# The next block's output product placed ahead of the last channel group of each feed-forward layer, with the sums kept in DRAM

## The chip, the core and the metric

The kernel runs on one core of a Trainium2 chip. A core has a matrix engine (PE, with weight loads listed as PEld), a vector engine (DVE), a scalar engine (ACT), a general engine (POOL), a queue engine that mostly issues DMAs (SP), and 16 DMA engines that all queues share. The engines run side by side, each in the order of its own instruction list, and wait for one another on semaphores. The metric is the device time of one execution in microseconds; lower is better.

## What is computed

One layer of a hybrid decoder trunk over 2048 tokens with 1024 features:

```python
h = rmsnorm(x, norm1_g) * (1 + sc1) + sh1
p = h @ w_in                                   # 3456 columns
y = concat([rglru(p), hgrn2(p), rwkv7(p)]) * mix_beta
x = x + g1 * (y @ w_out)                       # the output product
h = rmsnorm(x, norm2_g) * (1 + sc2) + sh2
x = x + g2 * ((silu(h @ w_gate) * (h @ w_up)) @ w_down)   # feed-forward, 2816 channels
return rmsnorm(x, final_g)
```

The three mixers (RG-LRU, HGRN2, RWKV-7) are recurrences along the tokens. They run in chunks, as many small operations on DVE and ACT with short matmuls between them.

## The kernel before, in words

Data lie feature-major: a tile has 128 features on the partitions and 512 tokens along the free side. The tokens are cut into four blocks (`NB`) of 512; the 1024 features are eight tiles (`KC`), the 2816 feed-forward channels 22 tiles (`NF`).

**Products.** Every f32 operand is split into a high part and a rest (`hh`/`hl` for activations, `wh`/`wl` for weights), and `project` (L261) makes three matmuls for each tile of the sum: high by high, high by rest, rest by high. An output product of one feature tile `d` is 8 x 3 = 24 matmuls, a down product over four channel tiles is 12, one over two channel tiles is 6. Weights come from DRAM by the SP queue into `wr` (3 buffers) and are split by ACT (`wh`) and DVE (`wl`, 4 buffers each). The products of `project` go to the PSUM banks `pd`, of which there are 3.

**Buffers that matter here.** `xs` is a tag with 12 buffers of one tile each (L135). From it come the loaded `x` tiles, the running sums `x1` of a block (eight tiles held from the output product to the final norm), squares and partial sums of squares, the scaled tiles in `make_h`, the gate results in `ffn_up`, and the loaded mixer outputs in `load_y`. `hh`/`hl` have 16 each.

**Order.** The program is written in Python and unrolled. A scheduler then orders each engine's instructions by a priority (levels `out`, `load`, `feed`, `mix`, `dense`, from first to last) as their inputs and buffers come free in its own model of the time. Tiles of one tag share its buffers; an instruction that first writes a tile needs a free buffer of the tag.

**Stages.** First the input projections and norms of all four blocks run, two blocks at a time (`w_in_products`), with the mixers of the first blocks interleaved. The last five projection columns (`IN_ORDER[-NT:]`) of blocks 2 and 3 end this stage. Then, for each block `b`:

- `w_out_products` (L1054): for each `d`, load the weight and the tile of `x`, make the product, add it to the tile with one DVE operation (`stt`), square it on ACT, and keep a sum of squares. At the end `rstd_of` (L354) turns the sum into the norm's factor: a split, matmuls with ones on PE, a logarithm and an exponential on ACT with a table load ahead of each.
- `ffn` (L1084): `make_h` (L388) scales and splits the eight tiles; then channel tiles are made by `ffn_up` (gate and up products) and consumed in groups of four, and a last group of two, by down products that add to `x1`. `load_y(b + 1)` (L1044) fetches the mixer outputs of the next block ahead of the last two groups; their split has the rest computed on POOL.
- `final_norm` of block `b` is deferred: it is called as `before()` inside the next block's `w_out_products`, behind the first product (L1063). It frees the eight `x1` tiles of block `b` as they are stored to `out`.

So in the order of PE the last down group of block `b` is followed by the output products of block `b + 1`, these by the norm's few matmuls, and these by the first up products of block `b + 1`, which need `make_h`.

Of the kernel before, what the change touches and what calls it, by code (L numbers as in the profile page):

```python
# [10 lines left out]
F = mybir.dt.float32  # L11
# [3 lines left out]
OP = mybir.AluOpType  # L15
PSUM = bass.MemoryType.PSUM

T = 2048
D = 1024
FF = 2816  # L20
TB = 512
KC = D // 128
NB = T // TB
NF = FF // 128
# [11 lines left out]
IN_ORDER = (25, 26, 19, 16, 20, 17, 22, 23, 7, 4, 10, 13, 0, 2, 21, 18, 24, 8, 5, 11, 14, 1, 3, 9, 6, 12, 15)  # L36
# [38 lines left out]
def hybrid_kernel(ctx, tc, x, par, ada_w, w_in, rgw, igw, w_up, a_up, g_up, w_out,  # L75
                  w_gate, w_upf, w_down, cst, msk, out):
    nc = tc.nc
    G, PE, SP = nc.gpsimd, nc.tensor, nc.sync
# [11 lines left out]
    @contextmanager  # L90
    def level(name):

        clock[levels[-1]] = tc.cur_priority
        levels.append(name)
        tc.cur_priority = clock[name]
        yield
        clock[name] = tc.cur_priority
        levels.pop()
        tc.cur_priority = clock[levels[-1]]
# [4 lines left out]
    def stt(o, a, s, b, op0, op1):  # L104
        return V.scalar_tensor_tensor(o, a, s, b, op0=op0, op1=op1)
# [19 lines left out]
    def bank(tag, bufs):  # L125
        return pp.tile([128, 512], F, name=tag, bufs=bufs)
# [17 lines left out]
    def pc(name, i=0):  # L144
        a, b = PCOLS[name]
        assert a + i < b
        return P[:, a + i:a + i + 1]
# [5 lines left out]
    def raw_w(src):  # L153
        w = dp.tile([128, TB], F, name="wr", bufs=3)
        i = SP.dma_start(w[:, :src.shape[1]], src)
        if w_after:
            order(i, w_after.pop())
        return w
# [30 lines left out]
    A2, B2, G1, G2 = Q2[:, 0:8], Q2[:, 8:16], Q2[:, 16:24], Q2[:, 24:32]  # L189
# [57 lines left out]
    def w_parts():  # L247
        return dp.tile([128, TB], R, name="wh", bufs=4), dp.tile([128, TB], R, name="wl", bufs=4)

    def load_w(src, fn):  # L250
        ws = []
        with level("load"):
            for c in range(0, src.shape[1], TB):
                n = min(TB, src.shape[1] - c)
                w = raw_w(src[:, c:c + n])
                hi, lo = w_parts()
                fn(w[:, :n], hi[:, :n], lo[:, :n])
                ws.append((hi, lo))
        return ws

    def project(h, *cols):  # L261

        ps = [bank("pd", 3) for ws in cols]
        tot = 3 * len(h)
        with level("dense"):
            for k, (hh, hl) in enumerate(h):
                c = slice((k % 4) * 128, (k % 4 + 1) * 128)
                for p, ws in zip(ps, cols):
                    wh, wl = ws[k // 4]
                    for n, (a, b) in enumerate(((wh, hh), (wh, hl), (wl, hh)), 3 * k):  # L270
                        PE.matmul(p, a[:, c], b, start=(n == 0), stop=(n == tot - 1))  # L271
                    now[0] += 0.68
                if k % (4 // len(ps)) == 4 // len(ps) - 1 or k == len(h) - 1:
                    tick()
        return ps
# [6 lines left out]
    def tick():  # L282
        for s in streams:
            while s["block"] < NB and now[0] >= s["at"]:
                step(s)
# [51 lines left out]
    def square_sum(s, t, k, tile=None, n=1):  # L337

        s, *last = s or (None,)
        if len(last) == n:  # L340
            if s is None:
                s = last.pop(0)
            else:
                (G if tile else V).tensor_add(s, s, last.pop(0))
        q = (tile or xs_)()
        if k == KC - 1:
            V.tensor_mul(q, t, t)
        else:
            squared[:] = [act(q, t, AF.Square)]
        return s, *last, q  # L350
# [18 lines left out]
    def load_x(src, b, k, tile=None):  # L369
        t = (tile or xs_)()  # L370
        load(t, src[k, :, b * TB:(b + 1) * TB])
        return t
# [39 lines left out]
    def drain(it):  # L412
        for _ in it:
            pass
# [3 lines left out]
    with level("feed"):  # L418
# [12 lines left out]
        rs = rstd_of(xsum)  # L431
# [20 lines left out]
    with level("mix"):  # L452
# [51 lines left out]
        for i in range(2):  # L504
            h, o = slice(64 * i, 64 * i + 64), slice(64 - 64 * i, 128 - 64 * i)
# [495 lines left out]
    def w_in_products(h, cols, side):  # L1001

        n = 0
        while n < len(cols):

            cs_ = cols[n:n + 2] if n == 0 and len(h) == 1 else cols[n:n + 1]
            ws = [W.pop(c) if c in W else load_w(w_in[c], split_v) for c in cs_]
            for i, b in enumerate(h):
                for j, (c, p) in enumerate(zip(cs_, project(h[b], *ws))):
                    with level("feed"):  # L1010
                        t = xs_()
                        if (n + i + j) % 2:
                            act(t, p)
                        else:
                            V.tensor_copy(t, p)
                        SP.dma_start(pd[c, :, b * TB:(b + 1) * TB], t)
                        stored.add((c, b))
                    next(side, None)
            n += len(cs_)
# [19 lines left out]
    for f in (mixers_a, mixers_b):  # L1039
        s = {"block": 0, "at": 0.0}  # L1040
# [3 lines left out]
    def load_y(b):  # L1044
        finish(b)
        ys = []
        for k in range(KC):
            t = load_x(yd, b, k)
            y = parts_()
            split(t, *y)  # L1050
            ys.append(y)
        return ys

    def w_out_products(b, ys, before):  # L1054
        x1, s = [], None
        for d in range(KC):
            ws = load_w(w_out[d], split_v)
            t = load_x(x, b, d)
            p, = project(ys, ws)
            with level("out"):  # L1060
                stt(t, p, G1[:, d:d + 1], t, OP.mult, OP.add)
            if d == 0:
                before()  # L1063
            s = square_sum(s, t, d)
            x1.append(t)
        return x1, rstd_of(s)

    def ffn_up(h, f):
        if f:
            p, = project(h, load_w(w_gate[f], split_v))  # L1070
        else:
            p, pu = project(h, load_w(w_gate[f], split_v), load_w(w_upf[f], split_v))
        t = xs_()
        with level("out"):
            act(t, p, AF.Silu)
        if f:
            pu, = project(h, load_w(w_upf[f], split_v))
        with level("out"):
            V.tensor_mul(t, pu, t)
        g = parts_()  # L1080
        split_v(t, *g)
        return g

    def ffn(b, x1, rs):  # L1084
        h = make_h(lambda k: x1[k], rs, A2, B2, "silu_and_others", over=False)
        gs, s, ys = [], None, None
        for f0 in range(0, NF, 4):
            n = min(4, NF - f0)
            while len(gs) < min(f0 + n + (2 if f0 + n + 2 >= NF else 1), NF):
                gs.append(ffn_up(h, len(gs)))  # L1090
            if len(gs) == NF and ys is None and b + 1 < NB:
                ys = load_y(b + 1)
            for d in range(KC):
                p, = project(gs[f0:f0 + n], load_w(w_down[d][:, f0 * 128:(f0 + n) * 128], split_v))
                with level("out"):
                    stt(x1[d], p, G2[:, d:d + 1], x1[d], OP.mult, OP.add)
                if f0 + n == NF:
                    s = square_sum(s, x1[d], d, n=1 if b + 1 < NB else 2)

        def final_norm():  # L1100
            rs = rstd_of(s)
            for d in range(KC):
                with level("dense"):
                    stt(x1[d], x1[d], pc("final_g", d), rs, OP.mult, OP.mult)
                    SP.dma_start(out[d, :, b * TB:(b + 1) * TB], x1[d])

        return ys, final_norm

    side = ada_rest()
    NH, NT = 4, 5  # L1110
    for b0 in range(0, NB, 2):
        h = {b0: h0}
        if b0 + 1 < NB:
            head, rest = IN_ORDER[:NH], IN_ORDER[NH:-NT]
            w_in_products(h, head, ahead)
            drain(ahead)
            h1 = {b0 + 1: norm1(b0 + 1)}
            w_in_products(h1, head, side)
            h.update(h1)
            ahead = x_stats(range(b0 + 2, min(b0 + 4, NB)), 1)  # L1120
            w_in_products(h, rest, chain(islice(side, 16), ahead, side))
            drain(ahead)
            w_in_products({b0: h[b0]}, IN_ORDER[-NT:], side)
            if b0 + 2 < NB:
                h0 = norm1(b0 + 2)
            w_in_products(h1, IN_ORDER[-NT:], side)
        else:
            w_in_products(h, IN_ORDER, side)
    drain(side)
    with level("feed"):  # L1130
        ys, before = load_y(0), lambda: None
    for b in range(NB):
        with level("feed"):
            ys, before = ffn(b, *w_out_products(b, ys, before))
    before()


# [54 lines left out]
```

## Time and profile before

| | us |
|---|---|
| median of 3 runs | 2858.53 |
| lowest, highest | 2855.87, 2863.30 |
| the profiled execution | 2862.48 |
| its span, first to last instruction | 2860.70 |

The profile is that of one execution, 3.95 us above the median of the runs; 1.8 us of it lie outside the span. Views of it group instructions by line and tile, list an engine's instructions in order of time, or give the busy time of each engine in a stretch. Nearly all instructions have line 69, a helper that counts them; they are told apart by their tiles. The DMA issues of the SP queue are listed with the time at which the queue issued them. The rows that matter stand in the prediction.

### The profile page before, as it was taken

How to read it: one execution, taken by the hardware profiler on the slowest of the kernel's cores; microseconds unless marked ns; L12 is line 12 of the kernel's file. 1: busy time of each engine (PE TensorE's matmuls, PEld its weight loads, DVE VectorE, ACT ScalarE, POOL GpSimd, SP SyncE). 2: the span in 40 equal slices, each digit the busy share in tenths (PEclk: the TensorE clock that was granted, in tenths of full speed). 3: DMA queues.
4: the chain of work that ended last, by engine and by line, in shares of the span. 5: the costliest groups of instructions: out<-in, count | busy, mean ns of one | idle time of the engine just before them, and what ended most of it. 6: DMA issues, size and time to landing. Idle time of an engine off the chain costs nothing. (4 is left out here: it accounts for less than half of the span.)

```text
span 2860.7 us, 41286 instructions
## 1 busy us (share of the span) xinstructions
PE 2732.2 (96%) x14842; PEld 2196.6 (77%) x14842; DVE 1932.6 (68%) x4112; ACT 1476.4 (52%) x2466; POOL 80.0 (3%) x67
## 2 busy tenths in 40 slices
PE   7999998999998999999989999999999999999998
PEld 6787776777876688877767877877778788788886
DVE  7677667867686875687877858778776445644435
ACT  4433854464547743666477456746773433433333
POOL 2000000000001000001000000010000001000000
PEclk9999999999999999999999999999999999999999
DMA  7553455544444242434333434335233333433332
GB/s 256 186 148 114 137 166 161 160 137 145 128 128 131 93 122 81 141 100 137 108 111 97 122 89 129 113 111 158 75 112 102 93 96 121 145 99 96 97 99 85
DMA packets 242590, 352.27 MB, mean 123 GB/s; under 512 B 72913, under 2 KB 78545, under 8 KB 242385
## 3 DMA queue, kind: packets, MB, share of 16 engines
q1 hardware_dynamic: 160144, 285.55, 31.9%
q10 hardware_dynamic: 82240, 64.09, 8.5%
q8 instruction: 117, 1.92, 0.3%
q14 instruction: 89, 0.72, 0.1%
HBM read 293.92 MB, written 55.62 MB: 122 GB/s over the span
## 5 line engine op out<-in xcount | busy, mean ns | idle before, releaser
L271 PE MATMUL pd<-hh,wh 128*128 128x512 f32 x3232 | 1295.1, 402 | 26.7 <-ACT hh L69 23.2
L271 PE MATMUL pd<-hl,wh 128*128 128x512 f32 x3232 | 1284.6, 398 | 5.0 <-DVE hl L69 3.9
L271 PE MATMUL pd<-hh,wl 128*128 128x512 f32 x3232 | 1282.4, 397 | 1.3 <-DVE wl L69 1.3
L69 ACT ACTIVATE wh<-wr 128x512 fp32r<-128x512 f32 (+1 forms) x752 | 464.0, 620 | 892.8 <-PE pd L271 719.6
L271 PEld LDWEIGHTS pd<-hh,wh 128*128 128x128 f32 x3232 | 613.5, 190 | 154.8 <-ACT hh L69 26.2
L271 PEld LDWEIGHTS pd<-hl,wh 128*128 128x128 f32 x3232 | 613.8, 190 | 136.2 <-DVE hl L69 8.9
L69 DVE TENSOR_TENSOR wl<-wr,wh 128x512 fp32r<-128x512 f32 (+1 forms) x752 | 510.8, 683 | 300.9 <-ACT wh L69 282.0
L271 PEld LDWEIGHTS pd<-hh,wl 128*128 128x128 f32 x3232 | 613.4, 190 | 130.3 <-issue 3.3
L69 ACT ACT_TABLE_LOAD x227 | 291.2, 1283 | 9.1 <-DVE tr L69 2.3
L69 DVE SCALAR_TENSOR_TENSOR xs<-pd,Q,xs 128x512 f32<-128x512 f32 x224 | 167.7, 748 | 141.6 <-PE pd L271 132.8
L69 DVE TENSOR_TENSOR th<-th 128x256 f32<-128x256 f32 (+8 forms) x349 | 155.0, 458 | 29.7 <-ACT th L69 23.3
L69 DVE TENSOR_TENSOR big<-big 128x30 f32<-128x30 f32 (+7 forms) x480 | 117.1, 244 | 10.2
L69 DVE TENSOR_TENSOR xs<-pd,xs 128x512 f32<-128x512 f32 x88 | 60.8, 691 | 87.2 <-PE pd L271 85.3
L69 ACT ACTIVATE xs<-pd 128x512 f32<-128x512 f32 x140 | 82.6, 590 | 69.4 <-PE pd L271 61.5
L69 ACT ACTIVATE th<-th 128x512 f32<-128x512 f32 (+2 forms) x153 | 93.3, 611 | 45.5 <-DVE th L69 25.8
L69 ACT ACTIVATE hh<-xs 128x512 fp32r<-128x512 f32 x120 | 74.4, 628 | 40.4 <-DVE xs L69 24.9
L69 ACT ACTIVATE hw<-big,we 64x64 f32<-64x64 f32 x192 | 66.1, 344 | 46.0 <-DVE big L69 43.1
L69 ACT ACTIVATE tr<-tr 128x512 fp32r<-128x512 f32 (+4 forms) x112 | 69.2, 626 | 13.9 <-DVE tr L69 12.9
L240 POOL TENSOR_TENSOR hl<-xs,hh 128x512 fp32r<-128x512 f32 x32 | 43.2, 1377 | 989.2 <-ACT hh L69 987.5
L69 DVE SCALAR_TENSOR_TENSOR big<-pc,we,hw 64x64 f32<-64x64 f32 x168 | 47.4, 282 | 32.5 <-PE pc L302 28.6
L69 DVE TENSOR_TENSOR tr<-tr 128x512 fp32r<-128x512 f32 (+2 forms) x80 | 54.7, 686 | 18.3 <-ACT tr L69 17.8
L69 DVE TENSOR_TENSOR hl<-xs,hh 128x512 fp32r<-128x512 f32 x88 | 60.7, 689 | 6.2 <-ACT hh L69 2.0
(185 smaller groups left out, 2290.7 us busy)
## 6 DMA issues: line engine op xcount, KB each, us to landing
wr<-in_w_gate SPq DMA_DIRECT2D x176, 256.0 KB, 2.6
wr<-in_w_upf SPq DMA_DIRECT2D x176, 256.0 KB, 2.6
wr<-in_w_down SPq DMA_DIRECT2D x160, 256.0 KB, 2.7
wr<-in_w_in SPq DMA_DIRECT2D x144, 256.0 KB, 3.4
pd<-xs SPq DMA_DIRECT2D x108, 256.0 KB, 3.1
xs<-in_x SPq DMA_DIRECT2D x72, 256.0 KB, 4.2
wr<-in_ada_w SPq DMA_DIRECT2D x64, 256.0 KB, 3.3
th<-pd ACTq DMA_DIRECT2D x64, 256.0 KB, 3.5
```

Of the source, the lines that this page charges most:

```text
L69: return f(*a, **k)
L240: G.tensor_sub(lo, src, hi.bitcast(F))
L271: PE.matmul(p, a[:, c], b, start=(n == 0), stop=(n == tot - 1))
```

## The change

The feed-forward channels are grouped 2, 4, 4, 4, 4, 4 in place of 4, 4, 4, 4, 4, 2. `ffn` makes all channel tiles and all groups but the last. In all blocks but the last, while the fifth group is added, each `x1` tile is stored to a DRAM tensor `xr`. Then `load_y` and `w_out_products` of the next block are called, and only then `ffn_last`, which makes the last group of the old block: it loads each tile back from `xr`, adds the down product, stores the result to a second DRAM tensor `xf`, and sums the squares. The final norm, now called in the next `ffn` behind its first three channel tiles, loads the tiles from `xf`, scales and stores them. For block 3 the tiles stay in place and no DRAM copy is made.

For block 0, which has no older block, the last five projection columns of block 3 are moved from the end of the projection stage to behind the output product of block 0.

```diff
@@ w_out_products
-    def w_out_products(b, ys, before):
+    def w_out_products(b, ys):
...
-            if d == 0:
-                before()
             s = square_sum(s, t, d)
@@
+    xr = tc.dram_tile([KC, 128, T], F, name="xr")
+    xf = tc.dram_tile([KC, 128, T], F, name="xf")
+    GROUPS = (2, 4, 4, 4, 4, 4)
+
+    def ffn_down(gs, f0, d):
+        p, = project(gs, load_w(w_down[d][:, f0 * 128:(f0 + len(gs)) * 128], split_v))
+        return p
+
+    def ffn(b, x1, rs, before):
         h = make_h(lambda k: x1[k], rs, A2, B2, "silu_and_others", over=False)
-        gs, s, ys = [], None, None
-        for f0 in range(0, NF, 4):
...
+        gs, f0 = [], 0
+        for i, n in enumerate(GROUPS[:-1]):
+            while len(gs) < min(f0 + n + 1, NF):
                 gs.append(ffn_up(h, len(gs)))
-            if len(gs) == NF and ys is None and b + 1 < NB:
-                ys = load_y(b + 1)
+            if i == 0:
+                before()
+            if i == len(GROUPS) - 2:
+                while len(gs) < NF:
+                    gs.append(ffn_up(h, len(gs)))
             for d in range(KC):
-                p, = project(gs[f0:f0 + n], load_w(...))
+                p = ffn_down(gs[f0:f0 + n], f0, d)
                 with level("out"):
                     stt(x1[d], p, G2[:, d:d + 1], x1[d], OP.mult, OP.add)
-                if f0 + n == NF:
-                    s = square_sum(s, x1[d], d, n=1 if b + 1 < NB else 2)
+                    if b + 1 < NB and i == len(GROUPS) - 2:
+                        SP.dma_start(xr[d, :, b * TB:(b + 1) * TB], x1[d])
+            f0 += n
+        return gs[f0:], f0
+
+    def ffn_last(b, x1, gs, f0):
+        s, ts_ = None, []
+        for d in range(KC):
+            t = load_x(xr, b, d) if b + 1 < NB else x1[d]
+            p = ffn_down(gs, f0, d)
+            with level("out"):
+                stt(t, p, G2[:, d:d + 1], t, OP.mult, OP.add)
+                if b + 1 < NB:
+                    SP.dma_start(xf[d, :, b * TB:(b + 1) * TB], t)
+            s = square_sum(s, t, d, n=1 if b + 1 < NB else 2)
         def final_norm():
             rs = rstd_of(s)
             for d in range(KC):
+                with level("feed"):
+                    t = load_x(xf, b, d) if b + 1 < NB else x1[d]
                 with level("dense"):
-                    stt(x1[d], x1[d], pc("final_g", d), rs, OP.mult, OP.mult)
-                    SP.dma_start(out[d, :, b * TB:(b + 1) * TB], x1[d])
-        return ys, final_norm
+                    stt(t, t, pc("final_g", d), rs, OP.mult, OP.mult)
+                    SP.dma_start(out[d, :, b * TB:(b + 1) * TB], t)
+        return final_norm
@@ the main program
             if b0 + 2 < NB:
                 h0 = norm1(b0 + 2)
-            w_in_products(h1, IN_ORDER[-NT:], side)
-        else:
-            w_in_products(h, IN_ORDER, side)
+                w_in_products(h1, IN_ORDER[-NT:], side)
     drain(side)
     with level("feed"):
-        ys, before = load_y(0), lambda: None
-    for b in range(NB):
-        with level("feed"):
-            ys, before = ffn(b, *w_out_products(b, ys, before))
+        x1, rs = w_out_products(0, load_y(0))
+        w_in_products(h1, IN_ORDER[-NT:], side)
+        before = lambda: None
+        for b in range(NB):
+            gs, f0 = ffn(b, x1, rs, before)
+            if b + 1 < NB:
+                x1, rs = w_out_products(b + 1, load_y(b + 1))
+            before = ffn_last(b, x1, gs, f0)
     before()
```

More of the change, by code (lines that the diff above doesn't have):

```diff
@@ L1082, in ffn_up @@
         return g
-    def ffn(b, x1, rs):
+    xr = tc.dram_tile([KC, 128, T], F, name="xr")
[5 more added lines that the diff above has]
+    def ffn(b, x1, rs, before):
         h = make_h(lambda k: x1[k], rs, A2, B2, "silu_and_others", over=False)
-        gs, s, ys = [], None, None
-        for f0 in range(0, NF, 4):
-            n = min(4, NF - f0)
-            while len(gs) < min(f0 + n + (2 if f0 + n + 2 >= NF else 1), NF):
+        gs, f0 = [], 0
+        for i, n in enumerate(GROUPS[:-1]):
+            while len(gs) < min(f0 + n + 1, NF):
                 gs.append(ffn_up(h, len(gs)))
-            if len(gs) == NF and ys is None and b + 1 < NB:
-                ys = load_y(b + 1)
+            if i == 0:
[3 more added lines that the diff above has]
+                    gs.append(ffn_up(h, len(gs)))
             for d in range(KC):
-                p, = project(gs[f0:f0 + n], load_w(w_down[d][:, f0 * 128:(f0 + n) * 128], split_v))
+                p = ffn_down(gs[f0:f0 + n], f0, d)
                 with level("out"):
                     stt(x1[d], p, G2[:, d:d + 1], x1[d], OP.mult, OP.add)
-                if f0 + n == NF:
-                    s = square_sum(s, x1[d], d, n=1 if b + 1 < NB else 2)
+                    if b + 1 < NB and i == len(GROUPS) - 2:
[12 more added lines that the diff above has]
+            s = square_sum(s, t, d, n=1 if b + 1 < NB else 2)
         def final_norm():
```

## The prediction, on record before the change was run

> **What bounds the kernel now.** First the page: the busy shares and the chain that ended last.
>
> ```profile
> span 2860.7 us, 41286 instructions
> PE 2732.2 (96%) x14842; PEld 2196.6 (77%) x14842; DVE 1932.6 (68%) x4112; ACT 1476.4 (52%) x2466; POOL 80.0 (3%) x67
> ```
>
> PE is busy for 96% of the span, so whatever the change can win is in the other 128.5 us. Next the view of busy time by stretches, cut at the stages (columns: stretch, length, PE, PEld, DVE, ACT, POOL busy, then granted PE clock, DMA share, GB/s).
>
> ```profile
> 860.00:880.00 20.00, 14.50 (x69) 10.68 (x68) 8.34 (x17) 17.61 (x33) 10.41 (x8) 0.91 0.48 159
> 940.00:956.00 16.00, 9.65 (x122) 5.91 (x122) 13.16 (x27) 14.28 (x18) 0.00 (x0) 0.77 0.26 85
> 1462.00:1476.00 14.00, 6.76 (x23) 3.98 (x23) 10.20 (x18) 13.79 (x22) 0.00 (x0) 0.69 0.25 77
> 2002.00:2018.00 16.00, 9.12 (x40) 6.76 (x41) 13.94 (x27) 13.44 (x22) 0.00 (x0) 0.86 0.22 73
> 2470.00:2490.00 20.00, 14.09 (x51) 9.72 (x50) 13.02 (x20) 11.56 (x16) 0.00 (x0) 0.83 0.18 58
> 2490.00:2846.00 356.00, 355.68 (x1570) 294.38 (x1568) 155.04 (x235) 112.85 (x186) 0.00 (x0) 1.00 0.31 93
> ```
>
> The last row is the feed-forward of block 3: PE has no gap in 356 us. The four rows above it stand behind the four output products: PE is idle there for 6.35, 7.24, 6.88 and 5.91 us, 26.4 us together, and the clock falls. This is the norm, which nothing covers. The timeline of the last one shows its parts (start, duration):
>
> ```profile
> 2477.27 0.39 PE L271 MATMUL pd<-hh,wl 128*128 128x512 f32 x1
> 2479.23 1.13 PE L365 MATMUL pd<-xs,aones 128*128 128x512 f32 x2 [1.57 <-DVE xs L69]
> 2484.61 1.22 PE L271 MATMUL pd<-hh,wh 128*128 128x512 f32 x2 [4.26 <-ACT hh L69]
> ```
>
> ```profile
> 2477.70 0.75 DVE L69 SCALAR_TENSOR_TENSOR xs<-pd,Q,xs 128x512 f32<-128x512 f32 x1 [0.83 <-PE pd L271]
> 2478.48 0.69 DVE L69 TENSOR_TENSOR xs<-xs 128x512 f32<-128x512 f32 x1
> ```
>
> ```profile
> 2482.39 0.63 ACT L69 ACTIVATE rstd<-rstd 128x512 f32<-128x512 f32 x1
> ```
>
> The last output product ends at 2477.5, its addition ends at 2478.45, the norm's factor is there at 2483.02, and the next up product starts at 2484.61: 1.6 us from factor to matmul for the first scaling and split. The first two matmuls after the gap take 1.22 us where the steady pitch is 0.2275 (353.05 over 1552, the next row); a stretch of 5 us holds 16 matmuls in place of 22, so the slow clock adds some 1.4 us.
>
> ```profile
> 2485.85 353.05 PE pd L271 x1552
> ```
>
> ```profile
> 2485.00:2490.00 5.00, 4.99 (x16) 3.51 (x16) 5.00 (x9) 3.06 (x5) 0.00 (x0) 0.71 0.00 0
> ```
>
> The ceiling of the change is therefore 26.4 + 4 x 1.4 = 32 us.
>
> **The change part by part.** The regrouping adds no matmul: six groups of eight products stay, 22 channels stay. The last group is now four wide, 8 x 12 x 0.2275 = 21.84 us of PE work, three times the norm's length. Whether it covers the norm depends on when its inputs and the buffers of the next step come, so I read how buffers are given out.
>
> *Buffers of one tag go out in program order.* The evidence is the mixer outputs, which need only an `xs` buffer:
>
> ```profile
> 634.26 0.33 ACTq L69 DMA_DIRECT2D yd<-tr  x1
> ```
>
> ```profile
> 861.36 0.33 SPq L1016 DMA_DIRECT2D pd<-xs  x1
> 861.74 0.43 SPq L164 DMA_DIRECT2D xs<-yd  x1
> 863.13 0.33 SPq L155 DMA_DIRECT2D wr<-in_w_out  x1
> 863.58 3.09 SPq L164 DMA_DIRECT2D xs<-yd  x6
> ```
>
> Block 0's outputs were written at 634 at the latest and no `x1` tile was held, yet seven of eight loads were issued only once the last projection tile, earlier in the program, had its copy out of PSUM. That is the gap at 860. So a later tile does not get a buffer, free or not, before every earlier tile of its tag has been written for the first time.
>
> *What this does to the new group.* In program order stand: the last square of the output product, then for each `d` the reload `t` from `xr` and the square of `t`, then the eight tiles of `make_h`. Hence the reload of `d + 1` comes behind the square of `d`, and that behind the addition of `d`. On the SP queue the store of `d` to `xf` becomes ready with the same addition and at a higher level, so it stands ahead of the reload. A store waits in its queue for its addition, as the kernel's end shows:
>
> ```profile
> 2851.91 5.39 DVE L69 SCALAR_TENSOR_TENSOR xs<-xs,P,rstd 128x512 f32<-128x512 f32 x8 [3.88 <-ACT rstd L69]
> ```
>
> ```profile
> 2852.68 4.97 SPq L1105 DMA_DIRECT2D out<-xs  x8
> ```
>
> Eight stores leave in step with eight additions, the first 0.02 us behind the first. Queued behind each waiting store are the reload of the next `d` and weight loads; DVE waits for the reload, and PE, with three banks, for DVE. This is a serial chain: addition, store issue, reload, addition. Its terms: an addition 0.75 (above), an issue 0.4, and a landing time. These rows have both, as minimum, median and maximum (tile `in_x` in the third and the last output product, `w_down` in the quiet last stage):
>
> ```profile
> L164 SPq DMA_DIRECT2D xs<-in_x x8: 328/356/448, 1944.6 to 1995.2; - x8
> ...
> DMA to landing us min/median/max: 2.9/3.4/4.6
> ```
>
> ```profile
> L164 SPq DMA_DIRECT2D xs<-in_x x8: 327/424/530, 2434.3 to 2467.7; - x8
> ...
> DMA to landing us min/median/max: 3.1/4.5/5.7
> ```
>
> ```profile
> L155 SPq DMA_DIRECT2D wr<-in_w_down x48: 327/328/328, 2526.0 to 2837.3; - x48
> ...
> DMA to landing us min/median/max: 2.0/2.7/3.8
> ```
>
> ```profile
> 1980.00:2000.00 20.00, 19.83 (x102) 1.00 0.55 176
> 2440.00:2460.00 20.00, 20.00 (x90) 1.00 0.83 253
> ```
>
> Each step of the chain moves a store, a reload and a weight, 768 KB in about 4.5 us or 170 GB/s. The third output product moves 176, the last one 253, the quiet stage 93 GB/s; so the row to take is the first, 3.4. One step is then 0.4 + 3.4 + 0.75 = 4.55 us against 2.73 us of matmuls, with ends 3.85 and 5.65 for landings of 2.7 and 4.5.
>
> At the junction of blocks 2 and 3: the first reload leaves when the last addition of the output product ends (2478.45), its own addition ends at 2482.6, the eighth at 2482.6 + 7 x 4.55 = 2514.45. The tiles of `make_h` come after the last square in program order, so the first up matmul follows 1.6 us later at 2516.05. Before it was 2484.61, and 21.84 us of old work are now done in between: 2516.05 - 2484.61 - 21.84 = **+9.6 us per junction**, +4.0 and +18.4 at the ends. The norm is hidden, but its place is taken by a longer wait. Three junctions: **+29** (+12 to +55).
>
> The Trainium skill (DMA: Bandwidth & Descriptors, Anatomy of one DMA) puts a DMA at about 2.0 us plus bytes over 436 GB/s, 2.6 us for such a tile as an estimate; by it a step is 3.75 us, the three junctions cost about 10, and the sum comes to 2865. The trace differs for most tiles in the busy stretches, 3.4 and 4.5, and agrees with the quiet 2.7. The same section says that waits sit on the issuing queue, not on the DMA engines, which agrees with the eight stores above.
>
> *Block 0's junction.* The moved columns, 5 x 24 x 0.2275 = 27.3 us, need no reload and cover the norm. `make_h` still follows the last column's copy, so some 2 to 3 us stay: **-4**, between 0 and -7.75 (6.35 + 1.4). The gap at 860 moves ahead of them and stays, since the mixer outputs still come behind the last earlier tile.
>
> *The final norm.* In the old place it held the `x1` buffers and made the next `x` loads late; PE lost 2.6 us there in block 0 (next rows) and under 1 in block 1. This goes: **-3** (0 to -3.4).
>
> ```profile
> 1420.00:1440.00 20.00, 18.55 (x91) 1.00 0.46 145
> 1440.00:1460.00 20.00, 18.88 (x95) 1.00 0.53 169
> ```
>
> In the new place eight loads, eight scalings at the lowest level and eight stores pass through the four `xs` buffers that `x1` leaves, and the fourth channel's tile is behind them in program order. Cover is the two-wide group (10.9), a gate product (5.5) and two banks (10.9): 27 us. The old stores of block 0 were spread over 41 us, those of block 1 over 35, those of block 2, with no mixers left, over 12:
>
> ```profile
> L1105 SPq DMA_DIRECT2D out<-xs x8: 332/344/402, 1409.0 to 1450.4; - x8
> ```
>
> ```profile
> L1105 SPq DMA_DIRECT2D out<-xs x8: 332/344/344, 1959.5 to 1994.3; - x8
> ```
>
> ```profile
> L1105 SPq DMA_DIRECT2D out<-xs x8: 343/400/477, 2443.6 to 2455.7; - x8
> ```
>
> If they spread as much again, 14 us come out at that place, 8 with the 35 us of the next block, and none with the 12 us of the last. I take **+4** (0 to +22), nearest the last block, because additions at the `out` level no longer compete there.
>
> *At nothing:* 96 new DMAs of 256 KB, by issue 35 us of a queue that PE does not wait for outside the chain; `xr` stores, ready well before their reload; the kernel's end, where the same additions and norm follow the last product; the two-wide group, whose additions (0.75) and half-size weight splits fit beside 1.37 us of matmuls per product unless the mixers take DVE.
>
> **Sum**: 29 - 4 - 3 + 4 = +26 on the profiled execution's 2862.5, 2888.5; that execution was 4 us above the median, so **2884 us**. Its own range is 2863 to 2920.
>
> **Rivals.** *(1) Both waits hidden: faster.* If the reloads were queued two or more `d` ahead, the group ran at PE's pitch, and if `make_h` got its buffers meanwhile, all gaps closed but some 2 us each: -24 for 32 - 8, -3 for the final norm: about 2831. For it: 21.84 us of cover against 7.1. Against: the loads at 861 to 866. It decides on one thing, whether a reload can be issued ahead of the store before it. Chance 0.14. *(2) Reloads run ahead, `make_h` does not.* Each gap shrinks to an addition, a square and 1.6 us, about 3: four times -4, -3, +4: 2843. Chance 0.12. *(3) The chain at quiet landings*, 3.85 us a step: +12 - 4 - 3 + 0, about 2864, hardly to be told from no change. For it the 2.7 row; against it, that row has only weights in flight. Chance 0.16. *(4) That the scheduler leaves the new group behind the norm*, so that nothing changes but the traffic, lies within (3).
>
> **Chances.** The forecast has 0.58. A measurement here can tell 0.3%, 8.6 us. Faster by more: all of (1) and most of (2), 0.25; within: the rest of (2) and most of (3), 0.17; slower: 0.58. The range leaves out the faster half of (1) and the top of the slow end, where the final norm stalls too: 2836 to 2916. As both signs hold chances, the forecast's own 2863 to 2920 stands beside it.
>
> **What would show it.** Right: in the last group of blocks 0 to 2 the additions stand about 4.5 us apart and wait for `xs<-xr`; on SP each reload follows the store of the `d` before; PE loses about 1.8 us per product and 10 to 15 us before the next up products, whose first scaling follows the group's last addition; behind block 0's output product PE is idle for 2 to 3 us. Wrong: additions 2.7 us apart, reloads ahead of the stores, or scalings of the next block inside the group. Then the time is below 2850.

## The result, and the profile after

The changed kernel takes 2892.5 us (median of 5 runs, 2891.0 to 2895.2), the kernel before beside it 2863.3 (5 runs). The ratio is 1.011, with a 95% interval of 1.0098 to 1.0122: slower by about 31 us (the two medians alone are 29 us apart).

The head of the page of the changed kernel:

```profile
span 2889.3 us, 41453 instructions
PE 2746.2 (95%) x14842; PEld 2202.9 (76%) x14842; DVE 1930.3 (67%) x4112; ACT 1498.7 (52%) x2485; POOL 81.3 (3%) x67
```

The matmul count is the same, yet PE is busy for 14.0 us more (2746.2 against 2732.2) and idle for 14.6 us more (143.1 against 128.5). Together that is the 28.6 us by which the span grew. To see where, the view of stretches, PE alone, from the last addition of an output product to the first up product behind it, for blocks 1, 2 and 3, and a fourth stretch around block 0's junction (columns: stretch, length, PE busy with its matmuls, granted clock, DMA share, GB/s). First the kernel before:

```profile
1464.90:1474.55 9.65, 2.45 (x7) 0.63 0.36 110
2004.88:2016.50 11.62, 5.02 (x25) 0.87 0.28 92
2477.70:2484.61 6.91, 1.13 (x2) 0.75 0.34 122
860.00:1000.00 140.00, 124.19 (x730) 0.95 0.35 111
```

The same for the changed kernel, where the first three also hold the last group, 21.84 us of matmuls at full clock:

```profile
1416.90:1466.53 49.63, 38.95 (x183) 0.90 0.53 167
1973.36:2021.24 47.88, 38.20 (x167) 0.91 0.47 149
2467.28:2508.97 41.69, 23.43 (x98) 0.86 0.55 171
860.00:1000.00 140.00, 135.11 (x803) 1.00 0.34 105
```

In the third stretch PE has nothing but the group's matmuls and the norm's two: 41.69 - 21.84 = 19.85 us stand beside the group's work, where it was 6.91. In the first two, mixer matmuls fill a part (183 and 167 matmuls for the group's 96). PE's idle time in the three is 10.68, 9.68 and 18.26 us against 7.20, 6.60 and 5.78: 19.0 us more. The granted clock is below 1.00 in all six stretches. The fourth row shows the other side: the columns moved behind block 0's output product cut the idle time there from 15.8 to 4.9 us, though not all of that is won: the wait at 860 now falls ahead of this stretch.

The timeline of DVE in the changed kernel, last group of block 2 (start, duration, idle time ahead and what ended it):

```profile
2467.28 0.75 DVE L69 SCALAR_TENSOR_TENSOR xs<-pd,Q,xs 128x512 f32<-128x512 f32 x1 [0.86 <-PE pd L271]
2471.70 0.75 DVE L69 SCALAR_TENSOR_TENSOR xs<-pd,Q,xs 128x512 f32<-128x512 f32 x1 [2.35 <-DMA xs<-xr]
2476.55 0.75 DVE L69 SCALAR_TENSOR_TENSOR xs<-pd,Q,xs 128x512 f32<-128x512 f32 x1 [1.65 <-DMA xs<-xr]
...
2506.03 0.75 DVE L69 SCALAR_TENSOR_TENSOR xs<-pd,Q,xs 128x512 f32<-128x512 f32 x1 [2.22 <-DMA xs<-xr]
...
2507.42 0.75 DVE L69 SCALAR_TENSOR_TENSOR xs<-xs,Q,rstd 128x512 f32<-128x512 f32 x1
```

The first row is the output product's last addition, the next three are the first, second and eighth of the group. Each waits for its reload, and they stand (2506.03 - 2471.70) / 7 = 4.90 us apart. The first scaling of the next block (last row) comes only behind them. The timeline of SP at the first two:

```profile
2472.48 0.33 SPq L1120 DMA_DIRECT2D xf<-xs  x1
2472.86 0.42 SPq L164 DMA_DIRECT2D xs<-xr  x1
...
2477.32 0.33 SPq L1120 DMA_DIRECT2D xf<-xs  x1
2477.69 0.43 SPq L164 DMA_DIRECT2D xs<-xr  x1
```

The store leaves 0.02 to 0.03 us behind the end of its addition, the reload of the next `d` 0.04 to 0.05 us behind the end of the store's issue. In blocks 0 and 1, beside the mixers, each reload but the first stands behind the store before it in the same way, and the additions are (1462.53 - 1421.57) / 7 = 5.85 and (2017.74 - 1977.64) / 7 = 5.73 us apart. The timeline of ACT and of PE show when the norm's factor was ready, and what PE waited for:

```profile
2471.98 0.63 ACT L69 ACTIVATE rstd<-rstd 128x512 f32<-128x512 f32 x1
```

```profile
2508.97 0.79 PE L271 MATMUL pd<-hh,wh 128*128 128x512 f32 x1 [13.64 <-ACT hh L69]
```

The factor lies unused from 2472.6 to 2507.4. When the group's additions end, PE has been idle for most of the 13.64 us.

### The profile page after: what moved, and what is told of

It reads as the page before. It is cut to its first block, busy times and chain, and to the rows that moved or that the text cites. A ratio compares the mean times of both kernels' runs of the same rounds, so it can differ in the third digit from the quotient of the medians.

```text
span 2889.3 us, 41453 instructions
## 1 busy us (share of the span) xinstructions
PE 2746.2 (95%) x14842; PEld 2202.9 (76%) x14842; DVE 1930.3 (67%) x4112; ACT 1498.7 (52%) x2485; POOL 81.3 (3%) x67
## 5 line engine op out<-in xcount | busy, mean ns | idle before, releaser
L69 DVE TENSOR_TENSOR th<-th 128x256 f32<-128x256 f32 (+6 forms) x349 | 155.0, 458 | 28.9 <-ACT th L69 24.4
L69 DVE TENSOR_TENSOR big<-big 128x30 f32<-128x30 f32 (+7 forms) x480 | 108.3, 226 | 10.3
L69 ACT ACTIVATE xs<-xs 128x512 f32<-128x512 f32 x77 | 48.2, 627 | 52.6 <-DVE xs L69 49.8
```

The lines of the kernel that those rows point to most:

```text
L69: return f(*a, **k)
```

## Experiments

The theory: a **chain** (store and reload in one queue) and the **late scaling** (`make_h` behind the last square) make the loss, and the moved columns win a little. Rivals: the added traffic costs the time by itself; the order of buffers, not the queue, makes the chain; the late scaling alone makes the loss. All ratios are to the kernel before, on the same chip. The chip is not the same in all experiments, so they are compared by their ratios.

**The store on another queue.** The stores to `xf` are issued by ACT, so that no reload stands behind one.

```diff
-                    SP.dma_start(xf[d, :, b * TB:(b + 1) * TB], t)
+                    A.dma_start(xf[d, :, b * TB:(b + 1) * TB], t)
```

> The stores to xf are issued from ACT's queue, all else as in the changed kernel. Theory (a store that waits in the SP queue holds the next reload behind it): SP no longer waits for the addition, the reload of the next d leaves earlier, additions in the last group come 3 to 4 us apart in place of 4.9, and the time falls from 2892 to 2868 to 2882; the scaling of the next block still follows the last addition. Rival (the 25 MB of added traffic slows the weights): the traffic is the same, so 2888 to 2896.

Measured: 2879.7, ratio 1.0064 (1.0043 to 1.0086). Some 13 us came back; the time is in the expected range, but not by the expected way, as the timelines show. SP's timeline in block 2:

```profile
2456.98 0.43 SPq L164 DMA_DIRECT2D xs<-xr  x1
...
2462.03 3.05 SPq L155 DMA_DIRECT2D wr<-in_w_gate  x2
2465.17 0.38 SPq L164 DMA_DIRECT2D xs<-xr  x1
2467.47 3.79 SPq L155 DMA_DIRECT2D wr<-in_w_upf  x2
2471.31 0.46 SPq L164 DMA_DIRECT2D xs<-xr  x1
```

And DVE's, the first addition of the group and the last:

```profile
2458.42 0.75 DVE L69 SCALAR_TENSOR_TENSOR xs<-pd,Q,xs 128x512 f32<-128x512 f32 x1 [1.84 <-DMA xs<-xr]
...
2495.07 0.75 DVE L69 SCALAR_TENSOR_TENSOR xs<-pd,Q,xs 128x512 f32<-128x512 f32 x1
```

Two things are to be seen. The second reload (2456.98) leaves before the first addition (2458.42), so it doesn't have to wait for that channel's square. And the third and fourth reload now stand behind pairs of weight loads that take 3 to 4 us to leave. The additions are (2495.07 - 2458.42) / 7 = 5.2 us apart, no better than before: in place of the store, other waiting instructions of the same queue stand ahead of the reload. That is not the whole of it: only the first, fourth and seventh addition are listed as waiting for their reload, and the fifth and sixth come behind a weight split that waited for PE.

The 13 us don't come from the group. From the output product's last addition to the group's eighth, DVE's timelines of the three junctions give 44.65, 46.01 and 40.57 us here and 45.63, 44.38 and 38.75 us in the changed kernel, 131 against 129 together. Where the gain comes from was not shown.

**Buffers of their own.** The reloads use the 16 buffers each of `hh` and `hl`. They can then be issued long before the group: block 2's leave from 2395 to 2406, its first addition is at 2445.98.

```diff
+    def own(d):
+        return lambda: dp.tile([128, TB], F, name=("hh", "hl")[d % 2], bufs=16)
...
-            t = load_x(xr, b, d) if b + 1 < NB else x1[d]
+            t = load_x(xr, b, d, own(d)) if b + 1 < NB else x1[d]
```

> The reloaded tiles come from the hh and hl buffers, of which four each are free there, and no longer from xs; queue, traffic and order of the program stay. Theory: the reloads no longer stand behind the squares, are all issued during the output product, and additions come 2.7 us apart; the scaling of the next block still follows the last square, so a gap of about 3 us stays per junction: 2845 to 2860. Rival (traffic): 2885 to 2895.

Measured: 2852.0, ratio 0.9975 (0.9962 to 0.9989). DVE's timeline of block 2, the group's second, third and eighth addition and the first scaling, then PE's first up product:

```profile
2448.84 0.74 DVE L69 SCALAR_TENSOR_TENSOR hl<-pd,Q,hl 128x512 f32<-128x512 f32 x1
2451.44 0.75 DVE L69 SCALAR_TENSOR_TENSOR hh<-pd,Q,hh 128x512 f32<-128x512 f32 x1 [0.46 <-PE pd L271]
...
2465.04 0.75 DVE L69 SCALAR_TENSOR_TENSOR hl<-pd,Q,hl 128x512 f32<-128x512 f32 x1 [0.52 <-PE pd L271]
...
2466.91 1.41 DVE L69 SCALAR_TENSOR_TENSOR xs<-xs,Q,rstd 128x512 f32<-128x512 f32 x2
```

```profile
2468.46 0.73 PE L271 MATMUL pd<-hh,wh 128*128 128x512 f32 x2 [3.46 <-ACT hh L69]
```

In block 2 the group runs at PE's pitch, 2.7 us, and waits for PE. The same bytes move, so the traffic by itself is not the price: the chain is, about 1.35% (1.011 to 0.9975) or 38 us. The three junctions, measured as above, take 80 us together in place of 129. The scalings still come behind the last addition, though by the count of tiles this version leaves two more `xs` buffers free, and PE waits 3.46 us for the first of them.

**The queue alone.** As the last, but each reload is ordered behind the store of the `d` before on SP. No `xs` buffer holds a reload back here.

```diff
             t = load_x(xr, b, d, own(d)) if b + 1 < NB else x1[d]
+            if ts_:
+                order(last_load[0], ts_.pop())
...
-                    SP.dma_start(xf[d, :, b * TB:(b + 1) * TB], t)
+                    ts_.append(SP.dma_start(xf[d, :, b * TB:(b + 1) * TB], t))
```

> As in the run with buffers of their own for the reloads, but each reload is put behind the store of the channel group before it on the SP queue, so that the queue alone can make the chain, and the order of buffers cannot. If the store in the queue is the chain, the additions of the last group stand 4.5 to 5 us apart again and the time is near that of the changed kernel: 2880 to 2895, with the kernel before at 2858. If the buffer that waits for the square is the chain, the additions stay 2.7 to 3 us apart and the time is 2848 to 2862. If either alone is enough, it is the first, though the run with the stores on ACT's queue kept 22 us of loss; if both share it, 2865 to 2880.

Measured: 2882.6, ratio 1.0077 (1.0053 to 1.0102). DVE's timeline of block 2, the first, second and eighth addition:

```profile
2460.97 0.75 DVE L69 SCALAR_TENSOR_TENSOR hh<-pd,Q,hh 128x512 f32<-128x512 f32 x1 [1.50 <-PE pd L271]
2465.31 0.75 DVE L69 SCALAR_TENSOR_TENSOR hl<-pd,Q,hl 128x512 f32<-128x512 f32 x1 [0.34 <-DMA hl<-xr]
...
2498.62 0.75 DVE L69 SCALAR_TENSOR_TENSOR hl<-pd,Q,hl 128x512 f32<-128x512 f32 x1 [2.25 <-DMA hl<-xr]
```

First to eighth, they are 5.4 us apart, and most of the loss is back. The three junctions take 128 us together, as long as in the changed kernel: the place behind the store in the queue is enough by itself.

**One reload ahead.** Buffers as in the changed kernel, but the reload of `d + 1` is listed ahead of the product, the store and the square of `d`.

```diff
+        tl = [load_x(xr, b, d) for d in range(1)] if b + 1 < NB else x1
         for d in range(KC):
-            t = load_x(xr, b, d) if b + 1 < NB else x1[d]
+            t = tl[d]
+            if b + 1 < NB and d + 1 < KC:
+                tl.append(load_x(xr, b, d + 1))
```

> The reload of channel group d + 1 is listed ahead of the product, the addition, the store and the square of d, still from the shared buffers. It then stands ahead of the store of d on SP, and waits only for a buffer. Eight of the twelve buffers are x1 of the next block, two are the sum and a square, two are left for reloads: the reload of d + 1 takes the buffer of d - 1, once the store of d - 1 has landed. Theory of the chain: two additions then take addition 0.75, issue 0.4, store about 3, issue 0.4, reload 3.4 to 3.9, some 8 us, so 4.0 to 4.3 us apart, and 2868 to 2882 with the kernel before at 2858. If one reload ahead is enough, the additions are 2.7 to 3.2 us apart and the time is 2848 to 2862. No gain: 2883 to 2895.

Measured: 2868.2, ratio 1.0032 (1.0015 to 1.0048). The time is the lower end of the first case. DVE's timeline, the first and the eighth addition of the group in block 0 and then in block 2:

```profile
1418.56 0.75 DVE L69 SCALAR_TENSOR_TENSOR xs<-pd,Q,xs 128x512 f32<-128x512 f32 x1 [0.17 <-DMA xs<-xr]
...
1446.51 0.73 DVE L69 SCALAR_TENSOR_TENSOR xs<-pd,Q,xs 128x512 f32<-128x512 f32 x1
...
2457.95 0.75 DVE L69 SCALAR_TENSOR_TENSOR xs<-pd,Q,xs 128x512 f32<-128x512 f32 x1 [2.04 <-DMA xs<-xr]
...
2478.58 0.75 DVE L69 SCALAR_TENSOR_TENSOR xs<-pd,Q,xs 128x512 f32<-128x512 f32 x1 [0.19 <-DMA xs<-xr]
```

The pitch is 4.0 us beside the mixers of block 0 (4.2 in block 1), as the first case had it, and 2.95 in block 2, as the second had it. My count of buffers was thus wrong for block 2 at least; which buffer each reload takes there was not traced. One reload listed earlier, with no buffer added, takes away some 70% of the loss (1.0110 to 1.0032).

**The scaling first.** `make_h` of the next block is called ahead of `ffn_last`; the reloads stay as changed.

```diff
...
             if b + 1 < NB:
                 x1, rs = w_out_products(b + 1, load_y(b + 1))
+                h = ffn_h(x1, rs)
             before = ffn_last(b, x1, gs, f0)
```

> make_h of the next block is called ahead of the last group of the old one, reloads still from xs. Theory: the scaling now runs as soon as the norm is there, but the reloads get their buffers only behind its eighth tile, some 15 us late, and the serial chain of about 4.9 us per d stays, partly covered by up products that cannot pass the group: 2890 to 2915. Rival (the late scaling was the whole loss, the chain is harmless): 2845 to 2865.

Measured: 2884.3, below what the theory had, ratio 1.0091 (1.0069 to 1.0113), not to be told from the changed kernel. DVE's timeline of block 2:

```profile
2462.30 0.75 DVE L69 SCALAR_TENSOR_TENSOR xs<-xs,Q,rstd 128x512 f32<-128x512 f32 x1 [3.27 <-ACT rstd L69]
...
2475.10 0.75 DVE L69 SCALAR_TENSOR_TENSOR xs<-pd,Q,xs 128x512 f32<-128x512 f32 x1 [0.30 <-DMA xs<-xr]
2479.61 0.75 DVE L69 SCALAR_TENSOR_TENSOR xs<-pd,Q,xs 128x512 f32<-128x512 f32 x1 [3.76 <-DMA xs<-xr]
```

The scalings run at once, but the first addition of the group now waits until 2475.1, behind all eight, and the chain follows. This edit takes one wait away and lengthens the other, so by itself it does not price the late scaling. That the late scaling alone is not the loss is shown by the reloads in buffers of their own, where the scalings are as late and the loss is gone.

**Both.** The reloads in their own buffers are listed ahead of `make_h`, and `make_h` ahead of the last group.

```diff
...
-            t = load_x(xr, b, d) if b + 1 < NB else x1[d]
+            t = x1[d]
...
+                tl = [load_x(xr, b, d, own(d)) for d in range(KC)]
+                h = ffn_h(x1, rs)
-            before = ffn_last(b, x1, gs, f0)
+            before = ffn_last(b, tl, gs, f0)
```

> Reloads from the hh and hl buffers, called ahead of make_h, and make_h called ahead of the last group. Theory: both waits gone, additions 2.7 us apart, the next up products follow the group without a gap; all four norms hidden: 2828 to 2845, faster than both kernels. Rival (traffic, or the final norm at its new place): 2880 or more.

Measured: 2837.1, ratio 0.9925 (0.9904 to 0.9945): 21 us faster than the kernel before and some 53 faster than the change as made. Additions and scalings alternate on DVE, and the view of stretches shows no gap in PE from the output product through the last group into the up products of block 3:

```profile
2430.00:2470.00 40.00, 39.99 (x175) 1.00 0.48 151
```

**Two parts of the change alone, in the kernel before.** The moved columns: the last five projection columns of block 3 are called behind block 0's output product.

```diff
-            w_in_products(h1, IN_ORDER[-NT:], side)
...
+        x1, rs = w_out_products(0, ys, before)
+        w_in_products(h1, IN_ORDER[-NT:], side)
...
```

> The kernel before with one part of the change alone: the last five projection columns of block 3 stand behind the output product of block 0. Theory: the norm of block 0 is covered, 4 to 7 us less than before (2856 to 2860 where before has 2863). Rival (the idle time of PE there is filled by mixers in either place): no change within 2 us.

Measured: 2853.9, ratio 0.9981 (0.9971 to 0.9991), so -5.4 us (-8.3 to -2.6). The regrouping:

```diff
-        for f0 in range(0, NF, 4):
-            n = min(4, NF - f0)
-            while len(gs) < min(f0 + n + (2 if f0 + n + 2 >= NF else 1), NF):
+        for f0, n in ((0, 2), (2, 4), (6, 4), (10, 4), (14, 4), (18, 4)):
+            while len(gs) < min(f0 + n + (4 if f0 + n + 4 >= NF else 1), NF):
```

The changed `while` line keeps what the kernel before does: all channel tiles are made ahead of the last two groups.

> The kernel before with the groups 2, 4, 4, 4, 4, 4 alone. Theory: the same matmuls and loads in another order, no change within 5 us. Rival (the two-wide group at the start, or the later fetch of the mixer outputs, costs): 5 to 15 us more.

Measured: 2851.7, ratio 0.9972 (0.9957 to 0.9986), so -8.0 us (-12 to -4), where nothing was expected. PE's timeline behind block 1's output product:

```profile
1451.80 0.49 PE L302 MATMUL pc<-big,KG 128*128 128x128 f32 x2 [1.16 <-DVE big L69]
...
1454.60 0.66 PE L302 MATMUL pc<-rs,GIQ 128*128 128x64 f32 x4 [1.07 <-ACT rs L69]
1456.84 1.13 PE L302 MATMUL pc<-big,BK 128*128 128x128 f32 x4 [1.58 <-ACT big L69]
1457.77 1.06 PE L302 MATMUL pm<-GIQ,big 128*128 128x128 f32 x4
```

Here mixer matmuls happen to stand in the norm's gap, and break it into idle times below 1.6 us. In the kernel before this gap cost 7.24 us (the row of 1462 to 1476). From the last addition to the first up product PE is idle here for 3.78, 3.60 and 5.79 us behind the output products of blocks 1, 2 and 3, against 7.20, 6.60 and 5.78. Together that is 6.4 us less, of the 9.3 us by which the idle time of the two profiled executions differs. Why the mixers fall there was not tried.

## Why the prediction was right

2884 was forecast and 2892.5 measured; inside the range and on the slow side, by the mechanism that had 0.58. One cause within that mechanism was wrong, and the size came out in part by luck. By its steps:

- **The chain**: right in its place and its links. Each reload but the first of a group left behind the store before it, the additions of block 2 waited for `xs<-xr`, and letting the reloads leave early won 1.35%, putting them back behind the stores alone lost 1.0%. Its step was undersized: 4.55 us by the landing of 3.4, against 4.90 in block 2 and 5.85 and 5.73 in blocks 0 and 1, where DVE and ACT also serve the mixers. Fewer additions there are listed as waiting for their reload, and what the mixers add to a step was not told apart. For block 2 the landing row of the reloads in the changed kernel (of all three blocks) gives a likely reason:

```profile
L164 SPq DMA_DIRECT2D xs<-xr x24: 319/424/1442, 1416.0 to 2502.8; - x24
...
DMA to landing us min/median/max: 2.4/3.9/8.4
```

  With 3.9 the sum 0.4 + 3.9 + 0.75 is 5.05, near the 4.90. (The 2.6 us estimated for such a tile from the Trainium skill, DMA: Bandwidth & Descriptors, Anatomy of one DMA, differs more: it is near the minimum of the row. That section gives its figures for DMAs issued by the general engine; these are SP's.) For the junction of blocks 2 and 3 the term +9.6 measured 41.69 - 21.84 - 6.91 = +12.9; for the other two +18.1 and +14.4, of which the mixers' matmuls give a part back. That PE would lose 1.8 us at each product was wrong: inside the group it loses 18.26 - 13.64 = 4.6 us in all, and the rest gathers in the one gap ahead of the up products, whose 13.64 us are within the 10 to 15 forecast.
- **The order of buffers** as the chain's second cause: the step "the reload of `d + 1` comes behind the square of `d`" failed. In the changed kernel itself the second reload leaves at 2472.86, before ACT begins the first square of the group at 2473.04. The store on ACT's queue let it leave ahead of the first addition, and the queue alone made the chain. The rows at 861 from which the step was read allow the queue as well: the seven loads stand behind the store of 861.36, for which SP waited 3.8 us by the view of waits. The place of the reload in its queue was the cause to name, with weight loads as a second thing that can stand ahead of it.
- **`make_h` behind the last square**: right in its place. The factor waited 35 us for use, the scalings stayed last even where by the count two more buffers were free, and listing `make_h` first took that away. That the order of buffers is the reason was not shown; the scheduler's priority of the additions would do the same. What the late scaling costs is a matter of what else stands: not measurable beside the chain, 0.5% without it (0.9975 to 0.9925, two versions that also list the reloads at different places).
- **Block 0's junction**, -4: measured -5.4, within the given bounds. Of the norm's gap less stays than the 2 to 3 us forecast, since mixer matmuls run between the last column and the first up product; PE's timeline of the changed kernel has this row at the latter:

```profile
943.93 0.73 PE L271 MATMUL pd<-hh,wh 128*128 128x512 f32 x2 [0.95 <-ACT hh L69]
```

- **The final norm**, -3 at the old place and +4 at the new: not run by itself. In block 2, at its new place, PE loses 0.56 us in 29 us, as the view of stretches of the changed kernel shows:

```profile
2536.00:2565.00 29.00, 28.44 (x123) 1.00 0.68 214
```

  So the +4, if it is there at all, lies in the blocks with mixers. This stays open.
- **At nothing**: the regrouping, which alone wins 8 us, was the wrong one. Since most of the idle time that it saves lies in the norm's gaps, which the change fills with other work, it cannot simply be added to the sum, and how much of it the changed kernel keeps was not measured.
- **The rivals**: the first was decided by the thing named, whether a reload can leave ahead of the store before it. With that alone the time was 2852, where the second rival had 2843; with `make_h` put first as well, 2837, where the first rival had 2831. The traffic alone is refuted as the price of the 31 us.

**The sum.** Span against span, +26 was forecast and +28.6 measured; most of the rest of the difference to 2892.5 is that the median of the kernel before is 4.8 us higher with these runs (2863.3) than with the three shown. So near a sum hides errors that partly cancel, and that they do is luck. The three junctions took 19.0 us of idle time and, if all of the longer busy time is put down to them, 14.0 us more, 33 together for the +29 of the forecast. The step was 0.35 us short, which is 7 x 0.35 = 2.5 us in block 2, and the slow clock inside the group had no price. In blocks 0 and 1 the step was over 1 us short, but mixer matmuls filled part of the longer wait, for which the forecast had no term. All other stretches together lost 4.4 us less idle time than before (14.6 - 19.0), for the -4, -3 and +4 of the forecast.

## What to carry to other kernels

Work that is to cover a wait must have its inputs queued before the wait starts: look at what stands ahead of its loads on the issuing queue, and whether that waits for the work itself. A store that waits for a result and a load that the next result needs make a chain on one queue, whose step is addition, issue and landing; list the load ahead of the store, with a buffer that is free. Where one wait hides another, undoing the hidden one alone can show nothing (`make_h` first: 1.0091 for 1.011), though it is worth something once the other is gone (0.9975 to 0.9925), so try both together before giving it up.

## What was not expected of the hardware

Half of the longer span is not idle time but PE at work for longer on the same matmuls. In the changed kernel the stretch that holds the end of the gap of 13.64 us, and the 11 us behind it, reads:

```profile
2500.00:2520.00 20.00, 11.03 (x36) 0.63 0.19 59
```

The granted clock is 0.63 on the mean of this stretch, gap included. The first matmul behind the gap takes 0.79 us, and the 36 matmuls take 11.03 us where the steady pitch of 0.2275 makes 8.2. The Trainium skill (TensorE: Matmul & The Clock Gate, Why this matters for your kernels) says to avoid idle gaps of PE above about 3 us; the trace agrees for this gap.

Heavy traffic does not by itself stop PE. With the reloads in their own buffers, these leave close behind the mixer outputs and among the `xr` stores, and the stretch of that kernel ahead of block 2's output product reads:

```profile
1880.00:1900.00 20.00, 11.02 (x42) 0.90 1.00 276
```

All 16 DMA engines are busy, and PE for only 11 of 20 us. But the changed kernel, in which no reload leaves there, has nearly the same row (first below), and the version with buffers of their own has a row ahead of block 3's output product, with no mixers left, in which nearly as much is moved and PE never stops (second):

```profile
1880.00:1900.00 20.00, 13.99 (x55) 0.84 0.96 255
```

```profile
2380.00:2400.00 20.00, 20.00 (x90) 1.00 0.83 264
```

So the mixer outputs and the `xr` stores bunch without the reloads, and beside the matmuls of the feed-forward 264 GB/s cost nothing. In the first stretch PE waits twice, 5.61 and 3.37 us, both times for mixer operations on DVE; the second of these had itself waited 4.86 us for a DMA. How much of the 9 us is the traffic's doing was not told apart.
